# Preparing weight factors one ring entry at a time, and the position scores of the later queries as two fp32r products

## The chip, the cores and the metric

The kernel runs on one core of one Trainium2 chip. The time is device microseconds of one execution; the number that counts is the median of three runs. The core's engines, as the profile names them: PE (TensorE, matrix products; PEld is its loading of the stationary operand), DVE (VectorE), ACT (ScalarE), POOL (GpSimd) and SP (SyncE, which here only issues the DMA transfers of weights). Each engine works off its own instructions in the order in which the build wrote them.

## The reference, cut to what matters

A decoder trunk of two layers over 256 positions of width 2048, all in float32. Layer 0 mixes by a gated short convolution, layer 1 by multi-head latent attention with 16 heads; behind each stands an MLP with squared ReLU and a hidden width of 8192. A layer norm follows every sub-layer.

```python
def sq_relu_mlp(x, w1, w2):
    return jnp.square(jax.nn.relu(x @ w1)) @ w2
...
def attend_block(args):
    qn, qp, blk = args
    s = (jnp.einsum("bqhd,bkhd->bhqk", qn, k_nope)
         + jnp.einsum("bqhr,bkr->bhqk", qp, k_pe)).astype(jnp.float32) * scale
    q_pos = blk * Q_BLOCK + jnp.arange(Q_BLOCK)
    mask = k_pos[None, :] <= q_pos[:, None]
    s = jnp.where(mask[None, None], s, -jnp.inf)
    p = jax.nn.softmax(s, axis=-1).astype(v.dtype)
    return jnp.einsum("bhqk,bkhd->bqhd", p, v)
```

A score has two parts: the head's own one over 128 features (qn, k_nope), and the position part over 64 rotated features (qp, k_pe), whose keys all heads share. The queries come in two blocks of 128; the first sees at most 128 keys, the later one 256.

## The kernel before

**Precision.** Nearly all products are made in the format fp32r, and an operand is held as two tiles of it: hi, a cast of the value (ACT, L127, in `split`), and lo, the value minus hi (DVE, L128). A product of two such pairs is three fp32r products: hi by hi, hi by lo, lo by hi (`dot`, L290 to L293; `mm_k1`, L223 to L225; `high` and `low`, L205 and L209). Some small products stay full F32; one of these stands in the trace as two records.

**The weight stream.** All weights pass once, in the order of the list `stream`, as entries of 128 x 1024. An entry is loaded by SP (L138) into a raw tile, of which there are five, and split into one of eight hi/lo pairs (the ring; RAW = 5, WA = 8). `take` (L176) hands out the next entries, and before that has later ones prepared by `prepare` (L141), as long as the entries ahead count at most LOOK = 5.

**Paired factors.** The MLPs cut the second product of the hidden eighths q = 1 to 6 (FAST; twelve paired chunks over both MLPs) by a scheme of seven products in place of eight (Strassen's kind). Such a factor comes from two loads and needs three ring entries and half a one: `_1` is the first raw tile, `_t` a difference of blocks (raw_t, L160), `_2` the second tile after a further difference (L163), and t4 another (L166) in a tile of its own. Before the change, `prepare` makes all of that in one go, and the factor counts three in the look-ahead: it is begun only when all three fit.

**A paired chunk** (`down_pairs`, from L630) takes, in this order: three paired factors s0, s1, s2 (products into banks ps_r); p0 and p1, one plain entry each, taken with a look-ahead of LOOK + 1; and four paired factors f0 to f3 (84 products of 128x512 into banks ps_f). Within one factor the seven products go in the order 3, 1, 5, 7, 2, 6, 4 (`FACTORS`), each three matmuls. The running sums go in and out of PSUM by copies of ACT: `put_back` (L609) stores a ps_r bank, `resumed` (L605) fills a ps_f bank with what has been summed so far. A bank of ps_f can be filled only when the bank's earlier sum has been stored. The copies and put-backs between the last s and f0 are issued while p0 and p1 are taken.

**Attention.** The heads go in four groups of four. `project` (L880) makes a group's keys, queries, rotated queries p4 (`rope`, L807, on DVE) and values from the latent tiles; `attend` (L914) does one head in three steps: scores (L923 the head's own part, L924 the position part, both F32) with the softmax up to its scaling; transposes and a copy; the product with the values. The rotated queries of two heads share a tile of 128 rows, 64 each. The position keys kpe hold, for each of the two, 64 rows of keys and 64 rows of zeros, so that one product of 128 rows takes one head's part. `together` runs the steps of three neighbouring heads, and the group's heads are interleaved with the next group's projections. Behind the last group, the first three units of the output product (`out_first`, ps_wo) fill in: BEHIND says how many of its 16 steps follow each of the seven last calls.

What stands in which order on an engine is otherwise settled by the build's scheduler, from the order of the code and the free tiles.

Of the kernel before, what the change touches and what calls it, by code (L numbers as in the profile page):

```python
# [10 lines left out]
F32 = mybir.dt.float32  # L11
F32R = mybir.dt.float32r
AF = mybir.ActivationFunctionType
ALU = mybir.AluOpType
AX = mybir.AxisListType

P = 128
W = 256 + 2
T = 256
# [22 lines left out]
HEAD = 4  # L42
# [2 lines left out]
TURNED = 2  # L45
LAG = 8
WO_G = 3
BEHIND = (2, 2, 2, 3, 2, 2, 3)

C_G, C_B, C_CW, C_QG, C_KG, C_END = 0, 64, 128, 176, 180, 184  # L50

# [2 lines left out]
def trunk(ctx: ExitStack, tc: tile.TileContext, xT, vecs, lead, w_first, w_in, w_out, w_kv, w_q, w_uk, w_uv,  # L54
          w_qn, w_qp, w_o, w1, w2, w2f, cosT, sinT, mask, ident, gb, out):
    nc = tc.nc
# [44 lines left out]
    class Banks:  # L101
# [15 lines left out]
        @classmethod  # L117
        def next(cls):
            cls.count += 1
            return (cls.count - 1) % (4 if cls.more is None else 8)  # L120

    state = {"split": 0, "next": 0}
    ready = {}

    def split(hi, lo, src):

        nc.scalar.copy(hi, src)  # L127
        nc.vector.tensor_tensor(lo, src, hi.bitcast(F32), ALU.subtract)  # L128

    def tiled(w):  # L130
        return w.rearrange("p (b c) -> p b c", c=P)
# [9 lines left out]
    def prepare(i):  # L141

        if len(stream[i]) == 1:
            raw = load_raw(i, stream[i][0])
            hi, lo = ready[i] = parts(i)
            split(hi, lo, tiled(raw))
            return
        r1, r2 = (load_raw(f"{i}_{j}", src) for j, src in enumerate(stream[i]))
        out = []

        def finished(r, name):
            hi, lo = parts(name)
            split(hi, lo, tiled(r))
            out.append((hi, lo))

        b22, (b21, b12) = r1[:, BW:], (r2[:, :BW], r2[:, BW:])
        finished(r1, f"{i}_1")
        t = raws.tile([P, 1024], F32, tag="raw", name=f"raw{i}_t")
        two = "p (a c) -> p a c"
        nc.vector.tensor_tensor(t.rearrange(two, a=2), b12.unsqueeze(1).to_broadcast([P, 2, BW]),  # L160
                                r1.rearrange(two, a=2), ALU.subtract)
        finished(t, f"{i}_t")
        nc.vector.tensor_tensor(b12, b22, t[:, :BW], ALU.subtract)  # L163
        finished(r2, f"{i}_2")
        t4 = r1[:, :BW]
        nc.vector.tensor_tensor(t4, b21, b12, ALU.subtract)  # L166
        f = state["fast"].tile([P, 2, BW], F32R, tag="t4", name=f"t4_{i}", bufs=2)
        split(f[:, 0, :], f[:, 1, :], t4)
        b1, t13, b2 = ([[v.rearrange("p b c -> p (b c)")[:, o:o + BW] for v in w] for o in (0, BW)] for w in out)
        ready[i] = {"11": b1[0], "22": b1[1], "21": b2[0], "T2": b2[1], "T1": t13[0], "T3": t13[1],  # L170
                    "T4": [f[:, 0, :], f[:, 1, :]]}

    def size(i):

        return 1 if len(stream[i]) == 1 else 3

    def take(halves=2, look=LOOK):

        i = state["next"]
        state["next"] += halves  # L180
        ahead = -sum(size(j) for j in range(i, i + halves))
        for j in range(i, len(stream)):
            ahead += size(j)
            if ahead > look:
                break
            if j >= state["split"]:
                prepare(j)
                state["split"] = j + 1
        return [ready.pop(i + j) for j in range(halves)]

    def psum(name, bank=None):

# [331 lines left out]
    for k0, k1 in pieces:  # L524
# [5 lines left out]
        for u in range(HEAD):  # L530
            hi, lo = ready[2 * u + half]
            split(hi[:, at, :], lo[:, at, :], w[:, :, u, :])
    state["split"] = 2 * HEAD
    nc.sync.dma_start(vec, vecs)

    zt = act.tile([P, NC, 2 * T], F32R, tag="b", name="z")
# [247 lines left out]
    with tc.tile_pool(name="att", bufs=1) as ap:  # L784
# [6 lines left out]
            nc.sync.dma_start(t, source)  # L791
        kpe = ap.tile([P, 2, T], F32, name="kpe")
        nc.gpsimd.memset(kpe, 0.0)
        rc = ap.tile([P, 2], F32, name="rc")
        rk = ap.tile([P, T], F32, name="rk")
        sc = ap.tile([P, 2], F32, name="sc")
# [2 lines left out]
        def rope(dst, src, rows):  # L799

            a = tmp.tile([P, T], F32, tag="sq", name="ropea")
            b = tmp.tile([P, T], F32, tag="evac", name="ropeb")
            nc.vector.tensor_tensor(a[rows], src[rows], cos_t[rows], ALU.mult)
            for s in range(rows.start, rows.stop, 32):
                d = s ^ 32
                nc.vector.tensor_tensor(b[d:d + 32], src[s:s + 32], sin_t[s:s + 32], ALU.mult)
            nc.vector.tensor_tensor(dst[rows], a[rows], b[rows], ALU.add)  # L807
# [41 lines left out]
        f = tmp.tile([P, T], F32, tag="fh", name="fpe", bufs=3)  # L849
        ln.weighted(next(pss), f)  # L850
        for j in range(2):
            rope(kpe[:, j, :], f, slice(64 * j, 64 * j + 64))
        for m in range(NK):
            ps = next(pss)
            if m == 0:
# [22 lines left out]
        with tc.tile_pool(name="att2", bufs=2) as a2, \  # L878
                tc.tile_pool(name="paux", bufs=1, space=PS) as paux:
            def project(g, box):  # L880

                k4, q4, p4, v4 = (t[g % 2] for t in (k2, q2, p2, v2))
                box.update(k=k4, q=q4, p=p4, v=v4)
                w = take()
                for j in range(4):
                    ps = psum("ps_k")
                    mm(ps, w, 4 * j, chl, NK)
                    nc.vector.tensor_tensor(k4[:, j, :], ps[:, :T], rk, ALU.mult)
                    yield
                w = take()  # L890
                for j in range(4):
                    ps = psum("ps_q")
                    mm(ps, w, 4 * j, qhl, NK)
                    nc.scalar.copy(q4[:, j, :], ps[:, :T])
                    yield
                if g == 0:
                    query_scale()
                for _ in range(4):
                    ln.normal(next(todo))
                w = take(1)  # L900
                for j in range(2):
                    ps = psum("ps_p")
                    mm(ps, w, 4 * j, qhl, NK)
                    rope(p4[:, j, :], ps[:, :T], slice(0, P))
                    yield
                w = take()
                for b in range(2):
                    ps = psum("ps_v")
                    for k in range(NK):
                        dot(ps, wide_rows(w[k // 2], k % 2), held(chl[k], b), k == 0, k == NK - 1)  # L910
                    nc.scalar.activation(v4[:, b, :], ps, AF.Copy, scale=rc[:, b:b + 1])
                    yield

            def attend(h, box):  # L914

                j = h % 4
                qn, kn = box["q"][:, j, :], box["k"][:, j, :]
                qp, kp = box["p"][:, j // 2, :], kpe[:, h % 2, :]
                S = paux.tile([P, 512], F32, tag="S", name=f"S_{h}", bufs=2)
                spans = ((0, P), (P, T))  # L920
                for b, (at, n) in enumerate(spans):
                    tok = slice(b * P, (b + 1) * P)
                    nc.tensor.matmul(S[:, at:at + n], qn[:, tok], kn[:, :n], start=True, stop=False)  # L923
                    nc.tensor.matmul(S[:, at:at + n], qp[:, tok], kp[:, :n], start=False, stop=True)  # L924
                pr = pr2[h % 2]
                mx = small.tile([P, 2], F32, tag="mx", name="mx")
                su = small.tile([P, 2], F32, tag="su", name="su")
                nc.vector.tensor_tensor(pr, S[:, :3 * P], mask_t, ALU.add)
                for b, (at, n) in enumerate(spans):
                    nc.vector.tensor_reduce(mx[:, b:b + 1], pr[:, at:at + n], AX.X, ALU.max)  # L930
                nc.vector.tensor_tensor(mx, mx, nsc, ALU.mult)
                for b, (at, n) in enumerate(spans):
                    nc.scalar.activation(pr[:, at:at + n], pr[:, at:at + n], AF.Exp, bias=mx[:, b:b + 1],
                                         scale=sc[:, b:b + 1], accum_out=su[:, b:b + 1])
                nc.vector.reciprocal(su, su)
                for b, (at, n) in enumerate(spans):
                    nc.vector.tensor_scalar(pr[:, at:at + n], pr[:, at:at + n], su[:, b:b + 1], None, ALU.mult)
                yield
                tp = paux.tile([P, 512], F32, tag="ta", name="tp")
                for n in range(3):  # L940
                    nc.tensor.transpose(tp[:, n * P:(n + 1) * P], pr[:, n * P:(n + 1) * P], id_t)
                pt = a2.tile([P, 3 * P], F32, tag="pt", name=f"pt_{h}")
                nc.scalar.copy(pt, tp[:, :3 * P])
                yield
                po = paux.tile([P, 512], F32, tag="tb", name="po")
                vv = box["v"]
                nc.tensor.matmul(po[:, :T], vv[:, 0, j * P:(j + 1) * P], pt[:, :T], start=True, stop=False)
                nc.tensor.matmul(po[:, P:T], vv[:, 1, j * P:(j + 1) * P], pt[:, T:], start=False, stop=True)
                put_split(oT[h], po[:, :T])
                yield  # L950
# [213 lines left out]
```

## Time and profile before

| | us |
|---|---|
| median of three runs | 2004.91 |
| lowest and highest | 2004.71, 2005.23 |
| the profiled execution | 2005.16 |
| its span, first to last instruction | 2003.4 |
| granted clock of TensorE over the span | 0.999 |

The times of single instructions come from one profiled execution, 2005.16 us long, of which the span covers 2003.4. A row of a group names the line, the engine, the operation, the tiles written and read, the shape and the count; behind the bar stand the total busy time in us, the mean of one in ns, and the idle time of the engine just before these instructions with what ended most of it. A row of the timeline begins with start and length in us, counted from the span's start; in brackets is the idle time before it and what ended it. Matmuls overlap, so the step from one start to the next, not the length, is what one costs. A row of waits gives the total, the number and the longest.

### The profile page before, as it was taken

The page shows a single profiled execution, that of the slowest core. Times are in us where ns is not written, and L with a number is a line of the kernel's source. Part 1 is how long each engine was busy: PE and PEld are TensorE (multiplying, and loading weights), DVE is VectorE, ACT ScalarE, POOL GpSimd, SP SyncE. Part 2 cuts the span into 40 slices and gives each one's busy share as a digit, 9 for nine tenths or more (in the row PEclk, how much of TensorE's full clock was granted, in tenths as well). Part 3 has the DMA queues.
Part 4 walks back from the last instruction along what each step waited for, and adds up shares of the span by engine and source line. Part 5 has one row for each costly group of instructions (what it writes and reads, how often), then busy time and mean ns, then how long its engine had stood idle before and what let it go on. Part 6 is the DMA issues. An engine that isn't in the chain of part 4 may idle for free.

```text
span 2003.4 us, 30132 instructions
## 1 busy us (share of the span) xinstructions
PE 1993.4 (100%) x11114; PEld 1737.5 (87%) x11114; DVE 1715.7 (86%) x2565; ACT 1347.5 (67%) x2142; POOL 2.3 (0%) x21
## 2 busy tenths in 40 slices
PE   9999999999999999999999999999999999999998
PEld 8888888988888888888889998898888888888886
DVE  8667667788999999989978988777899999999986
ACT  6444445586877787877756755558677778887771
POOL 0000000000000000000000000000000000000000
PEclk9999999999999999999999999999999999999999
DMA  8666666564647465574854543656464646656483
GB/s 314 210 189 188 188 190 189 184 193 146 223 164 244 147 231 197 187 247 133 281 173 158 170 140 128 195 183 196 147 233 147 233 159 219 218 181 231 152 276 118
DMA packets 106851, 385.84 MB, mean 193 GB/s; under 512 B 11856, under 2 KB 12624, under 8 KB 106448
## 3 DMA queue, kind: packets, MB, share of 16 engines
q1 hardware_dynamic: 106560, 383.79, 58.8%
q8 instruction: 87, 1.43, 0.3%
q14 instruction: 60, 0.49, 0.1%
q10 hardware_dynamic: 144, 0.13, 0.0%
HBM read 381.78 MB, written 2.10 MB: 192 GB/s over the span
## 4 chain that ended last, share of the span: by engine, by line
PE 90%; DVE 7%; issue 2%; ACT 1%; DMA 0%; DVEq 0%
PE ps_u L205 21%; PE ps_l L205 13%; PE ps_u L209 11%; PE ps_l L209 7%; PE ps_r L292 4%; PE ps_r L290 4%; PE ps_r L293 4%; PE ps_d L292 3%; PE ps_d L290 3%; PE ps_d L293 3%; DVE lo L128 2%; PE ps_w L239 2%; PE ps_w L238 2%; DVE lo_t L128 2%; PE ps_w L237 2%
## 5 line engine op out<-in xcount | busy, mean ns | idle before, releaser
L128 DVE TENSOR_TENSOR lo<-raw,hi 128x1024 fp32r<-128x1024 f32 x710 | 860.5, 1219 | 191.1 <-ACT hi L127 109.4
L127 ACT CAST hi<-raw 128x1024 fp32r<-128x1024 f32 x710 | 742.3, 1051 | 241.4 <-PE ps_l L205 97.5
L205 PE MATMUL ps_u<-xhl,hi 128*128 128x512 f32 x1792 | 622.8, 393 | 0.0
L209 PE MATMUL ps_u<-xhl,lo 128*128 128x256 f32 x1792 | 498.6, 280 | 0.0
L205 PEld LDWEIGHTS ps_u<-xhl,hi 128*128 128x128 f32 x1792 | 334.5, 187 | 74.2 <-ACT acc L588 0.2
L209 PEld LDWEIGHTS ps_u<-xhl,lo 128*128 128x128 f32 x1792 | 338.2, 189 | 1.7
L205 PE MATMUL ps_l<-xhl_a,hi 128*128 128x512 f32 x704 | 244.1, 393 | 0.0
L209 PE MATMUL ps_l<-xhl_a,lo 128*128 128x256 f32 x704 | 195.4, 279 | 0.0
L205 PEld LDWEIGHTS ps_l<-xhl_a,hi 128*128 128x128 f32 x704 | 132.1, 188 | 29.9
L127 ACT CAST hi_t<-raw_t 128x1024 fp32r<-128x1024 f32 x84 | 88.6, 1055 | 84.6 <-DVE raw_t L160 69.0
L209 PEld LDWEIGHTS ps_l<-xhl_a,lo 128*128 128x128 f32 x704 | 131.9, 188 | 0.2
L160 DVE TENSOR_TENSOR raw_t<-raw,raw 128x1024 f32<-128x1024 f32 x84 | 102.2, 1217 | 2.9 <-DMA raw<-in_w2f_dram 2.9
L128 DVE TENSOR_TENSOR lo_t<-raw_t,hi_t 128x1024 fp32r<-128x1024 f32 x84 | 102.3, 1218 | 1.4 <-ACT hi_t L127 0.9
L290 PE MATMUL ps_d<-hi,h 128*128 128x512 f32 x256 | 99.9, 390 | 0.0
L292 PE MATMUL ps_d<-lo,h 128*128 128x512 f32 x256 | 99.7, 389 | 0.0
L293 PE MATMUL ps_d<-hi,h 128*128 128x512 f32 x256 | 99.7, 389 | 0.0
L205 PE MATMUL ps_l<-z,hi 128*128 128x512 f32 x240 | 82.4, 391 | 0.0
L239 PE MATMUL ps_w<-xd,hi 128*128 128x258 f32 x256 | 72.8, 284 | 0.0
L237 PE MATMUL ps_w<-xd,hi 128*128 128x258 f32 x256 | 72.3, 282 | 0.0
L238 PE MATMUL ps_w<-xd,lo 128*128 128x258 f32 x256 | 72.3, 282 | 0.0
L205 PE MATMUL ps_l<-oT,hi 128*128 128x512 f32 x208 | 71.3, 391 | 0.0
L704 ACT ACTIVATE fp<-fp 128x256 f32<-128x256 f32 x96 | 40.0, 417 | 43.9 <-DVE fp L348 43.1
(286 smaller groups left out, 3890.5 us busy)
## 6 DMA issues: line engine op xcount, KB each, us to landing
raw<-in_w_dram SPq DMA_DIRECT2D x344, 512.0 KB, 4.5
raw<-in_w2f_dram SPq DMA_DIRECT2D x168, 512.0 KB, 4.0
raw<-in_w_in_dram SPq DMA_DIRECT2D x88, 512.0 KB, 4.2
raw<-in_w_out_dram SPq DMA_DIRECT2D x32, 512.0 KB, 3.7
raw<-in_w_o_dram SPq DMA_DIRECT2D x32, 512.0 KB, 4.1
raw<-in_w_kv_dram SPq DMA_DIRECT2D x10, 512.0 KB, 4.3
raw<-in_w_q_dram SPq DMA_DIRECT2D x8, 512.0 KB, 4.2
raw<-in_w_uk_dram SPq DMA_DIRECT2D x8, 512.0 KB, 3.9
```

The costliest lines, as they stand in the source:

```text
L127: nc.scalar.copy(hi, src)
L128: nc.vector.tensor_tensor(lo, src, hi.bitcast(F32), ALU.subtract)
L160: nc.vector.tensor_tensor(t.rearrange(two, a=2), b12.unsqueeze(1).to_broadcast([P, 2, BW]), r1.rearrange(two, a=2), ALU.subtract)
L205: nc.tensor.matmul(ps, w[blk // 8][0][:, blk % 8, :], x, start=first, stop=False)
L209: nc.tensor.matmul(ps[:, :T], w[blk // 8][1][:, blk % 8, :], x[:, :T], start=False, stop=last)
L237: nc.tensor.matmul(ps[:, :W], hi, x[k][:, :W], start=k == 0, stop=False)
L238: nc.tensor.matmul(ps[:, :W], lo, x[k][:, :W], start=False, stop=False)
L239: nc.tensor.matmul(ps[:, :W], hi, x[k][:, W:], start=False, stop=k == NC - 1)
L290: nc.tensor.matmul(ps, x[0], w[0], start=first, stop=False, skip_group_check=onto)
L292: nc.tensor.matmul(ps[:, at], x[0], w[1][:, at], start=False, stop=False, skip_group_check=onto)
L293: nc.tensor.matmul(ps, x[1], w[0], start=False, stop=last, skip_group_check=onto)
L704: nc.scalar.activation(f, f, AF.Relu)
```

## The change

It has three parts.

1. `prepare` becomes a generator that stops after each ring entry, and `take` counts the look-ahead by entries: a paired factor is begun as soon as its first entry fits, and carried on entry by entry. What is begun is kept in a dictionary.
2. For the later query block, the F32 position product is replaced by two fp32r products. A new tile s4 holds, for each head, hi of the rotated queries in the head's own 64 rows, and lo in the other 64. It is multiplied by kph, in which both halves of the rows hold hi of the keys (hi by hi and lo by hi in one product), and by kpl, lo of the keys in the head's own rows and zeros in the others (hi by lo). The first block keeps its F32 product.
3. BEHIND moves a step of the output product from the fourth call to the sixth.

```diff
-BEHIND = (2, 2, 2, 3, 2, 2, 3)
+BEHIND = (2, 2, 2, 2, 2, 3, 3)
...
             split(hi, lo, tiled(raw))
+            yield
             return
...
         finished(r1, f"{i}_1")
+        yield
         t = raws.tile([P, 1024], F32, tag="raw", name=f"raw{i}_t")
...
         finished(t, f"{i}_t")
+        yield
         nc.vector.tensor_tensor(b12, b22, t[:, :BW], ALU.subtract)
         finished(r2, f"{i}_2")
...
+        yield
...
+    begun = {}
...
         for j in range(i, len(stream)):
-            ahead += size(j)
-            if ahead > look:
-                break
-            if j >= state["split"]:
-                prepare(j)
-                state["split"] = j + 1
-        return [ready.pop(i + j) for j in range(halves)]
+            for step in range(size(j)):
+                ahead += 1
+                if ahead > look:
+                    return [ready.pop(i + k) for k in range(halves)]
+                if j < 2 * HEAD:
+                    continue
+                steps = begun.setdefault(j, [prepare(j), 0])
+                if steps[1] == step:
+                    next(steps[0])
+                    steps[1] += 1
+        return [ready.pop(i + k) for k in range(halves)]
...
+        kph = ap.tile([P, T], F32R, name="kph")
+        kpl = ap.tile([P, 2, T], F32R, name="kpl")
+        nc.gpsimd.memset(kpl.bitcast(F32), 0.0)
...
         for j in range(2):
-            rope(kpe[:, j, :], f, slice(64 * j, 64 * j + 64))
+            rows = slice(64 * j, 64 * j + 64)
+            rope(kpe[:, j, :], f, rows)
+            split(kph[rows], kpl[rows, j, :], kpe[rows, j, :])
...
                     rope(p4[:, j, :], ps[:, :T], slice(0, P))
+                    for e in range(2):
+                        own, other = slice(64 * e, 64 * e + 64), slice(64 - 64 * e, 128 - 64 * e)
+                        src, hi = p4[own, j, P:], s4[own, 2 * j + e, :]
+                        nc.scalar.copy(hi, src)
+                        nc.vector.tensor_tensor(s4[other, 2 * j + e, :], src, hi.bitcast(F32), ALU.subtract)
...
-                    nc.tensor.matmul(S[:, at:at + n], qp[:, tok], kp[:, :n], start=False, stop=True)
+                    if b == 0:
+                        nc.tensor.matmul(S[:, at:at + n], qp[:, tok], kp[:, :n], start=False, stop=True)
+                    else:
+                        nc.tensor.matmul(S[:, at:at + n], box["s"][:, j, :], kph, start=False, stop=False)
+                        nc.tensor.matmul(S[:, at:at + n], box["s"][:, j, :], kpl[:, h % 2, :], start=False, stop=True)
```

More of the change, by code (lines that the diff above doesn't have):

```diff
@@ L120, in next @@
             return (cls.count - 1) % (4 if cls.more is None else 8)
-    state = {"split": 0, "next": 0}
+    state = {"next": 0}
     ready = {}
@@ L532, in trunk @@
             split(hi[:, at, :], lo[:, at, :], w[:, :, u, :])
-    state["split"] = 2 * HEAD
     nc.sync.dma_start(vec, vecs)
@@ L882, in project @@
                 k4, q4, p4, v4 = (t[g % 2] for t in (k2, q2, p2, v2))
-                box.update(k=k4, q=q4, p=p4, v=v4)
+                s4 = a2.tile([P, 4, P], F32R, tag="s4", name=f"s4_{g}")
+                box.update(k=k4, q=q4, p=p4, v=v4, s=s4)
                 w = take()
```

## The prediction

> **What bounds the kernel now.** I read the page's heads first, then what PE waited for, then the windows of the stretches in which it waited.
>
> ```profile
> span 2003.4 us, 30132 instructions
> PE 1993.4 (100%) x11114; PEld 1737.5 (87%) x11114; DVE 1715.7 (86%) x2565; ACT 1347.5 (67%) x2142; POOL 2.3 (0%) x21
> ...
> PE 90%; DVE 7%; issue 2%; ACT 1%; DMA 0%; DVEq 0%
> ```
> ```profile
> PE ps_f L292 <- DVE lo_t L128: 2.4, 3, 1.0
> ```
> ```profile
> L292 PE MATMUL ps_f<-lo_t,forms 128*128 128x512 f32 x96 | 38.6, 402 | 3.2 <-DVE lo_t L128 2.4
> L290 PE MATMUL ps_f<-hi_t,forms 128*128 128x512 f32 x96 | 37.6, 392 | 0.3 <-ACT hi_t L127 0.3
> ```
>
> TensorE sets the end: 1993.4 of 2003.4 us busy. So an edit counts only by taking matmul time away or by ending a wait of PE. One wait repeats: the ps_f products, in the paired chunks of the MLPs, wait for lo_t, the low part of a factor's middle ring entry. How much it costs is best read from the twelve stretches of ps_f products, one for each paired chunk (the fields are window, its length, PE busy with the count of matmuls, clock, DMA share, GB/s):
>
> ```profile
> 514.80:541.80 27.00, 19.20 (x84) 1.00 0.63 226
> 598.00:625.00 27.00, 19.77 (x84) 1.00 0.56 177
> 682.80:709.80 27.00, 19.50 (x84) 1.00 0.57 191
> ...
> 933.80:960.80 27.00, 19.94 (x84) 1.00 0.54 171
> ...
> sum 324.00, PE 234.13; mean PE 19.51
> ```
>
> The same 84 matmuls take 19.20 in the first stretch and more in the third. A matmul that is held shows part of its wait as busy time, so the excess is 234.13 − 12 × 19.20 = 3.7, plus the idle 3.2 + 0.3 of the two groups above: **7.2 us in all**. The clock is 1.00 everywhere; only waiting explains it. The third stretch is the common form, an excess of 0.3 busy and about 0.1 idle; the second and the one at 933.80 are the large ones (about 1.6 and 2.0 with their idle).
>
> Where the wait comes from shows in VectorE and ScalarE of the third stretch:
>
> ```profile
> 682.27 1.22 DVE L160 TENSOR_TENSOR raw_t<-raw,raw 128x1024 f32<-128x1024 f32 x1
> 683.52 0.69 DVE L163 TENSOR_TENSOR raw<-raw,raw_t 128x512 f32<-128x512 f32 x1
> 685.79 1.22 DVE L128 TENSOR_TENSOR lo<-raw,hi 128x1024 fp32r<-128x1024 f32 x1 [1.57 <-PE ps_r L292]
> ...
> 700.72 1.22 DVE L128 TENSOR_TENSOR lo_t<-raw_t,hi_t 128x1024 fp32r<-128x1024 f32 x1
> ```
> ```profile
> 682.16 1.65 ACT L605 COPY ps_f<-sums 128x512 f32<-128x512 f32 x3
> 683.72 1.09 ACT L609 COPY acc<-ps_r 128x512 f32<-128x512 f32 x2
> 684.67 1.08 ACT L127 CAST hi<-raw 128x1024 fp32r<-128x1024 f32 x1
> 685.62 1.09 ACT L127 CAST hi_t<-raw_t 128x1024 fp32r<-128x1024 f32 x1
> ```
> ```profile
> 701.48 0.39 PE L290 MATMUL ps_f<-hi_t,forms 128*128 128x512 f32 x1
> 701.99 0.50 PE L292 MATMUL ps_f<-lo_t,forms 128*128 128x512 f32 x1
> ```
>
> VectorE idles 1.57 us ahead of 685.79, the first split of factor f1. The page blames PE; the timing says ScalarE: the cast that feeds the split starts at 684.67, behind three copies into ps_f and two put-backs. After that VectorE never rests until 700.72, where it makes lo_t of f3 and is about 0.3 too late (701.48 to 701.99 where 0.23 is the undisturbed step). A factor costs VectorE four operations of 1.14 (1.22 with 0.08 of overlap) and three of about 0.65, 6.5 in all, while PE uses one up in 19.20 / 4 = 4.8; so whatever VectorE loses ahead of f1 arrives at f3.
>
> **The change, part 1: factors by one ring entry.** The look-ahead now fills to the entry, so f1's first two entries are asked for before the copies. The built order says what that moves. On ScalarE: copy into ps_f1, cast f1_1, cast f1_t, two ps_f copies, two put-backs (r2, r4), cast f1_2, cast t4, put-backs r22 and r3. On VectorE the subtraction that starts f2 (raw_t) moves ahead of f1's third split. SyncE's loads and PE's products stay in place here, and nothing is added, so the cost is only in the moves.
>
> Step by step in the third stretch. Five copies fill 682.16 to 684.67, 0.50 each; a cast takes 0.95 (684.67 to 685.62). Cast f1_1 now ends at 682.16 + 0.50 + 0.95 = 683.6. VectorE is then held by its own L163, whose successor could start at 683.52 + 0.7 = 684.2. The split moves from 685.79 to 684.2: gain 1.57, all of the idle time. Next on VectorE: two splits at 1.14, the t4 subtraction at 0.6 (687.1), then raw_t of f2, which needs f2's second load:
>
> ```profile
> L138 SPq DMA_DIRECT2D raw<-in_w2f_dram x1: 327/327/327, 682.4 to 682.4; - x1
> ...
> DMA to landing us min/median/max: 5.1/5.1/5.1
> ```
>
> It lands at 682.4 + 5.1 = 687.5 and gives 0.4 back. So lo_t of f3 comes 1.2 earlier; it was 0.4 late; **the stall goes, with 0.75 spare**. VectorE's other work is no smaller, it only starts sooner.
>
> The two large stretches have less to gain:
>
> ```profile
> 602.14 1.23 DVE L128 TENSOR_TENSOR lo<-raw,hi 128x1024 fp32r<-128x1024 f32 x1 [1.33 <-ACT hi L127]
> ...
> 938.34 1.22 DVE L128 TENSOR_TENSOR lo<-raw,hi 128x1024 fp32r<-128x1024 f32 x1 [1.33 <-ACT hi L127]
> ```
>
> Idle there is 1.33; against 1.6 and 2.0 about 0.3 and 0.7 remain. Everything that is late next is the put-back of r22, now behind two casts and t4: in the third stretch 682.16 + 0.50 + 2 × 0.95 + 4 × 0.50 + 0.95 + two steps of 0.5 = 688.5. PE needs that bank at the product "4" of f0:
>
> ```profile
> 689.92 0.39 PE L290 MATMUL ps_f<-t,h 128*128 128x512 f32 x1
> ```
>
> Slack 1.4, so nothing in the eight common stretches (ps_f5 and ps_f7 shift by 1.9 and are ready at 685.1 and 685.6, before the third and fourth products). In the two large stretches I take it as covered by the 0.3 and 0.7 already left standing. Part 1: −7.2 + 1.0 = **−6.2**. Bounds: −7.2, if nothing is left; above, 0, if no stall goes (rivals).
>
> **Part 2: the position scores of the later query block.** Per head one full F32 128x256 product (L924) becomes two fp32r products of 128x256. The trace has no fp32r product of these tiles; the nearest rows follow it immediately:
>
> ```profile
> 1151.56 0.59 PE L924 MATMUL S<-kpe,kqva 128*128 128x256 f32 x2
> 1151.80 0.47 PE L223 MATMUL ps_k<-lat,lo 128*128 128x256 f32 x1
> 1152.11 0.28 PE L224 MATMUL ps_k<-lat,hi 128*128 128x256 f32 x1
> 1152.23 0.29 PE L225 MATMUL ps_k<-lat,hi 128*128 128x256 f32 x1
> ```
>
> An F32 product is two records. From its start to L224 are 0.55, which hold it and one fp32r product at 0.12 (1152.11 to 1152.23): 0.43 for the pair. The new pair is 2 × 0.12 = 0.24. Saved: 0.19 × 16 heads = **−3.1**, from −3.2 at the best to 0, if a change of number format on PE costs what it saves. I take the near end, because PE is full here and the same step from F32 to fp32r stands in the rows.
>
> Added: for each head a cast and a subtraction of 64x128 (32 instructions), two splits of 64x256, and one fill on POOL, which has nothing else. Nearest rows by size:
>
> ```profile
> L127 ACT CAST hi<-lead 128x128 fp32r<-128x128 f32 x16 | 3.6, 294 | 0.0
> ```
> ```profile
> L128 DVE TENSOR_TENSOR lo<-lead,hi 128x128 fp32r<-128x128 f32 x16 | 3.6, 283 | 0.0
> ```
>
> So about 16 × 0.28 + 2 × 0.4 = 5.3 on VectorE and as much on ScalarE, over 110 us. VectorE looks full there (columns: PE, PEld, DVE, ACT, POOL busy, clock, DMA share, GB/s), but PE is as full and does not wait for it:
>
> ```profile
> 1100.00:1130.00 30.00, 30.00 (x226) 28.88 (x225) 29.70 (x65) 19.67 (x35) 0.00 (x0) 1.00 0.65 212
> 1130.00:1240.00 110.00, 109.98 (x736) 101.91 (x736) 93.40 (x240) 67.78 (x155) 0.00 (x0) 1.00 0.37 120
> ```
>
> VectorE is ahead, preparing weights, and in the second window it has 16.6 us free: the 5.3 are covered by that. Without the cover they cost up to 5.3. The tightest place is the first group:
>
> ```profile
> 1121.09 0.42 DVE L807 TENSOR_TENSOR kqva<-ropea,ropeb 128x256 f32<-128x256 f32 x1
> ```
> ```profile
> 1124.19 0.59 PE L924 MATMUL S<-kpe,kqva 128*128 128x256 f32 x2
> ```
>
> Rotation done at 1121.5; two heads' splits one after the other, 2 × (0.29 + 0.28) = 1.15, end at 1122.7: slack 1.5. I count 0.
>
> The row on fp32r steps has a rule against it. The Trainium skill ("TensorE: Matmul & The Clock Gate", part 3, "The mechanism", the list of what overlaps) says that a weight load overlaps a running matmul only where their row groups differ; here all 128 rows are used, so each added product would show its load. By that rule part 2 would be a loss (third rival); the trace disagrees with it in ps_k, where loads of 0.19 disappear in steps of 0.12.
>
> **Part 3: BEHIND.** The sum stays at 17. In the built order five output units plus one product stand before the last head's final part in both versions, as three and two before and two and three after. A unit is three products of 512 and three of 256, 3 × (0.23 + 0.12) = 1.05, and moving one past a wait costs or gains at most that. I take **0**, bounds ±1.05.
>
> **Sum.** 2003.4 − 6.2 − 3.1 = 1994.1. The profiled execution took 2005.16, so 1.76 lie around the span: 1995.9. It stands 0.25 above the median of 2004.91, so on the median's scale **1995.6 us**. This case's own range is 1993.8 to 1999.2 (all of the stall and half of BEHIND below; above, half the attention gain gone and a further 0.2 per stretch left).
>
> **The rivals.**
>
> *ScalarE's row is longer than I add up* (0.07). If r22 comes 2.0 later than 688.5, it holds product "4" by 0.6 in the eight common stretches: 4.8, **2000.4**. For it: two casts now stand ahead of that put-back, and each waits for VectorE. Against: the 1.4 of slack.
>
> *VectorE blocked by f2's load* (0.05), the slow side. The subtraction for f2 now stands ahead of f1's third split; if its load is late, all four factors are. Spare 0.75 beyond 5.1 means that it starts to cost at 5.9 us from issue to landing, and each microsecond more costs ten in ten stretches. It is slower by 0.2% from (2008.9 − 1995.6) / 10 + 5.9 = 7.2 us on; at 7.7 it gives **2013.6**. For it, the longest landing of the stage; against, the median of these loads:
>
> ```profile
> DMA to landing us min/median/max: 3.3/4.3/7.7
> ```
> ```profile
> raw<-in_w2f_dram SPq DMA_DIRECT2D x168, 512.0 KB, 4.0
> ```
>
> *The new products show their weight loads* (0.03): a pair then takes 2 × (0.19 + 0.12) = 0.62 in place of 0.43, so +3.0 where I have −3.1: **2001.7**. For it, PEld's own duration; against, that loads of the same length vanish in the steps of 0.12 above:
>
> ```profile
> L224 PEld LDWEIGHTS ps_k<-lat,hi 128*128 128x128 f32 x64 | 12.2, 191 | 0.2
> ```
>
> *The order gains nothing* (0.06): VectorE starts f1 earlier but waits again for a cast further on, and lo_t is as late as before. Only part 2 is left: **2001.8**. For it: VectorE and ScalarE hand each factor over four times (three entries and t4); against: ScalarE has over 30% free.
>
> **Chances.** The forecast has 0.79. This kernel's measurement can tell about 0.2% from no change: faster means below 2000.9, slower above 2008.9. Faster: 0.79 and 0.04 of the first rival, 0.83; same: 0.03 + 0.03 + 0.06 = 0.12; slower 0.05. The range 1993.8 to 2000.6 takes in the first rival's middle and leaves out 0.06 + 0.03 + 0.05 and half of the first, under 0.2.
>
> **What would show it.** In the profile after, each window of ps_f should have 19.2 to 19.3 busy, with about 19.5 and 19.9 left at 598 and 933 at the most; the wait for lo_t should fall from 3.2 to under 1; VectorE's idle time before f1's first split should vanish. The position row of 128x256 should read as two products 0.12 apart. A new wait of ps_f for ACT's put-back, or of VectorE for the load of f2, would show the first or second rival. It is wrong if ps_f still has 19.5 in the common stretches.

## The result, and the profile after

The changed kernel takes 1999.24 us (median of 7 runs, 1998.47 to 2000.01), the one before 2004.71 in the same comparison (7 runs, 2003.03 to 2006.03): a ratio of 0.9973, with a 95% interval of 0.9964 to 0.9983. That is 5.5 us, where the prediction had 9.3, and 3.6 above its forecast of 1995.6. The prediction names two upper ends: the time lies 0.04 over the one of its own case, 1999.2, and inside the one that also takes in the first rival, 2000.6. The profiled execution took 1998.59, its span is 1996.8, 6.6 under the span before. Of the two parts that were to pay, one did and one hardly did.

The heads of the page, and what PE waits for now (engine, operation, what it waited for; total in us, times, longest):

```profile
span 1996.8 us, 30215 instructions
PE 1987.7 (100%) x11114; PEld 1736.6 (87%) x11114; DVE 1720.5 (86%) x2583; ACT 1355.6 (68%) x2160; POOL 2.7 (0%) x22
```
```profile
PE po L972 <- DVE oT L363: 2.2, 3, 1.1
PE offset L1083 <- DVE udiag L1081: 1.2, 1, 1.2
...
PE ps_f L300 <- ACT acc L618: 0.4, 1, 0.4
```

The wait of ps_f for lo_t has left the list; one of 0.4 for a put-back is new, and one of 2.2 in the attention: the product po (probabilities by values) waits for VectorE's oT.

The twelve windows of ps_f, with the fields as before:

```profile
...
681.00:708.00 27.00, 19.20 (x84) 1.00 0.63 226
...
930.80:957.80 27.00, 19.75 (x84) 1.00 0.57 192
...
sum 324.00, PE 231.19; mean PE 19.27
```

The reckoning of before, 231.19 − 12 × 19.20 + 0.4, leaves 1.2 of 7.2 us: **the factor part gained 6.0**. What the move did is seen in the third stretch, on ScalarE and VectorE:

```profile
680.23 0.61 ACT L614 COPY ps_f<-sums 128x512 f32<-128x512 f32 x1
680.75 1.07 ACT L127 CAST hi<-raw 128x1024 fp32r<-128x1024 f32 x1
681.70 1.06 ACT L127 CAST hi_t<-raw_t 128x1024 fp32r<-128x1024 f32 x1
682.65 1.12 ACT L614 COPY ps_f<-sums 128x512 f32<-128x512 f32 x2
...
686.12 1.10 ACT L618 COPY acc<-ps_r 128x512 f32<-128x512 f32 x2
```
```profile
681.15 0.69 DVE L166 TENSOR_TENSOR raw<-raw,raw_t 128x512 f32<-128x512 f32 x1
681.85 1.23 DVE L128 TENSOR_TENSOR lo<-raw,hi 128x1024 fp32r<-128x1024 f32 x1
...
696.54 1.22 DVE L128 TENSOR_TENSOR lo_t<-raw_t,hi_t 128x1024 fp32r<-128x1024 f32 x1
```
```profile
688.12 0.39 PE L300 MATMUL ps_f<-t,h 128*128 128x512 f32 x1
```

The casts of f1_1 (680.75) and f1_t stand right behind the copy at 680.23, ahead of the other two copies and of the put-backs. VectorE goes from L166 (L163 before) to f1's first split without a pause. lo_t of f3 starts at 696.54 and is done by 697.8; PE uses it at 699.91. The put-back of r22 (the first of the two from 686.12) is done 1.4 before PE starts the product "4" at 688.12.

The attention: how long the products po take, from the first head's to the last one's. The first row is the kernel before, the second the changed one:

```profile
L947 PE MATMUL po<-pt,kqva x32: 377/378/454, 1140.5 to 1233.3; 128*128 128x256 f32 x32
```
```profile
L972 PE MATMUL po<-pt,kqva x32: 377/378/455, 1135.8 to 1228.9; 128*128 128x256 f32 x32
```

1233.3 − 1140.5 = 92.8 before, 93.1 after. The scores of thirteen heads lie in this stretch, those of three ahead of it; thirteen should have taken 13 × 0.19 = 2.5 off it, and instead it is 0.3 longer. What they saved on PE was there. One head's scores, before (first fence, with the rows of the prediction) and after:

```profile
1151.12 0.60 PE L923 MATMUL S<-kqva 128*128 128x256 f32 x2
```
```profile
1146.24 0.60 PE L944 MATMUL S<-kqva 128*128 128x256 f32 x2
1146.49 0.47 PE L948 MATMUL S<-kph,s 128*128 128x256 f32 x1
1146.80 0.29 PE L949 MATMUL S<-kpl,s 128*128 128x256 f32 x1
1146.92 0.28 PE L233 MATMUL ps_k<-lat,lo 128*128 128x256 f32 x1
1147.04 0.28 PE L234 MATMUL ps_k<-lat,hi 128*128 128x256 f32 x1
```

From the head's own part to the second ps_k product are 1152.11 − 1151.12 = 0.99 before and 1147.04 − 1146.24 = 0.80 after: 0.19 a head, as predicted. The two new products start 0.31 apart, not 0.12 as the prediction had it; but before the change the first two products behind the F32 pair read so too (1151.80 and 1152.11), so only the sum over these rows tells. The saving went back to the waits of po. Where the first of them arises, on VectorE and PE:

```profile
1175.43 1.22 DVE L128 TENSOR_TENSOR lo<-raw,hi 128x1024 fp32r<-128x1024 f32 x1
1176.68 0.60 DVE L924 TENSOR_TENSOR s<-kqva,s 64x128 fp32r<-64x128 f32 x2
1177.32 2.36 DVE L128 TENSOR_TENSOR lo<-raw,hi 128x1024 fp32r<-128x1024 f32 x2
1179.71 0.42 DVE L363 TENSOR_TENSOR oT<-po,oT 128x256 fp32r<-128x256 f32 x1
```
```profile
1179.36 0.28 PE L235 MATMUL ps_k<-lat,hi 128*128 128x256 f32 x1
1180.28 0.67 PE L972 MATMUL po<-pt,kqva 128*128 128x256 f32 x2 [0.64 <-DVE oT L363]
```

The product po has one PSUM bank. Before it can be written for the next head, VectorE must have read it for the low part of oT, and that subtraction stands behind three weight splits and the new pair (L924). At the same head before the change, two weight splits stood there, and po did not wait:

```profile
1179.86 2.35 DVE L128 TENSOR_TENSOR lo<-raw,hi 128x1024 fp32r<-128x1024 f32 x2
1182.24 0.42 DVE L353 TENSOR_TENSOR oT<-po,oT 128x256 fp32r<-128x256 f32 x1
```
```profile
1185.30 0.60 PE L947 MATMUL po<-pt,kqva 128*128 128x256 f32 x2
```

There the subtraction starts 3.06 ahead of the product. In the changed kernel PE was due for the product one step after 1179.36, at 1179.48, and the subtraction starts 0.23 behind that: it is 3.3 later, counted from when PE needs it.

The 2.2 of idle are not the whole price, since a held product shows part of its wait as busy time: the pair of po is recorded at 0.67 where it was held and at 0.60 before the change. By the stretch the waits cost 0.3 + 2.5 = 2.8.

And VectorE is not short of time (columns: PE, PEld, DVE, ACT, POOL busy, clock, DMA share, GB/s):

```profile
1130.00:1240.00 110.00, 107.78 (x725) 99.46 (x725) 98.15 (x252) 72.51 (x169) 0.00 (x0) 1.00 0.37 116
```

Before, PE had 109.98 and VectorE 93.40 here: VectorE does 4.8 more and still has 11.9 free, and PE idles 2.2 more.

### The profile page after: what moved, and what is told of

The parts are those of the page before. It is cut to its first block, busy times and chain, and to the rows that moved or that the text cites. A ratio compares the mean times of both kernels' runs of the same rounds, so it can differ in the third digit from the quotient of the medians.

```text
span 1996.8 us, 30215 instructions
## 1 busy us (share of the span) xinstructions
PE 1987.7 (100%) x11114; PEld 1736.6 (87%) x11114; DVE 1720.5 (86%) x2583; ACT 1355.6 (68%) x2160; POOL 2.7 (0%) x22
## 4 chain that ended last, share of the span: by engine, by line
PE 94%; DVE 5%; ACT 1%; issue 1%; DVEq 0%; ACTq 0%
PE ps_u L215 20%; PE ps_l L215 13%; PE ps_u L219 10%; PE ps_l L219 7%; PE ps_f L300 4%; PE ps_f L302 4%; PE ps_f L303 4%; PE ps_r L302 4%; PE ps_r L303 4%; PE ps_r L300 4%; PE ps_d L300 3%; PE ps_d L302 3%; PE ps_d L303 3%; PE ps_w L249 2%; PE ps_w L248 2%; PE ps_w L247 2%
```

## The experiments

The theory (A): the factor part took away the stall of ps_f and touched nothing else; the scores save some 3 us on PE, but the splits they add on VectorE delay its reading of the po bank, and PE waits. The rivals B to F stand in the expectations, each with what it would show.

**The factor part alone.** The changed kernel with the scores and BEHIND of before.

```diff
+BEHIND = (2, 2, 2, 3, 2, 2, 3)
...
-            split(kph[rows], kpl[rows, j, :], kpe[rows, j, :])
...
-                        nc.scalar.copy(hi, src)
-                        nc.vector.tensor_tensor(s4[other, 2 * j + e, :], src, hi.bitcast(F32), ALU.subtract)
...
+                    nc.tensor.matmul(S[:, at:at + n], qp[:, tok], kp[:, :n], start=False, stop=True)
```

> Only the preparation by ring entry is taken over; scores and BEHIND stay as before. Theory A (the factor part took the stall of ps_f away and touched nothing else): 6.0 us under before, each ps_f window at 19.2 busy but the one near 935 (about 1.0 left), no wait of the product po for oT. Rival B (the new order of take also moves weight splits ahead of oT in the attention, and that makes PE wait there): about 3.6 us under before, with 2.2 us of wait of po for oT.

Measured: 2000.43 against 2004.93, ratio 0.9979 (0.9970 to 0.9987), so 4.5 us with the interval from 2.6 to 6.0, where 6.0 was expected. In its profile neither po nor the transposes wait, and the stretch of po is 1229.3 − 1136.5 = 92.8, as before. What is left in ps_f is 1.8 (231.62 busy, 0.6 idle, most of it one wait of 0.5 for the put-back), against 1.2 in the changed kernel.

So the attention's waits do not come from the factors (B falls), and most of the gain does.

**The scores alone.** The kernel before with part 2 of the change.

```diff
+            split(kph[rows], kpl[rows, j, :], kpe[rows, j, :])
...
+                        nc.scalar.copy(hi, src)
+                        nc.vector.tensor_tensor(s4[other, 2 * j + e, :], src, hi.bitcast(F32), ALU.subtract)
...
+                        nc.tensor.matmul(S[:, at:at + n], box["s"][:, j, :], kph, start=False, stop=False)
+                        nc.tensor.matmul(S[:, at:at + n], box["s"][:, j, :], kpl[:, h % 2, :], start=False, stop=True)
```

> Only the position scores are taken over. Theory A (16 x 0.19 saved on PE, but the added splits of the rotated queries push the low part of oT back on VectorE, behind weight splits, and the next product po waits 2.2 to 2.4 us in all): 0.7 us under before, with waits of po for oT; the waits for lo_t stay at 3.2. Rival B (the waits come from the factor part): 3.1 us under before and no wait of po.

Measured: 2003.74 against 2004.93, ratio 0.9995 (0.9986 to 1.0004): no difference that can be told from none. Its list of waits has both:

```profile
PE ps_f L292 <- DVE lo_t L128: 2.9, 4, 1.0
PE po L963 <- DVE oT L353: 2.2, 3, 1.1
```

The same 2.2, three times, at the same heads, with the old factors and the old BEHIND, and a stretch of 1233.0 − 1139.9 = 93.1. The scores bring their waits along.

**BEHIND alone.**

```diff
-BEHIND = (2, 2, 2, 3, 2, 2, 3)
+BEHIND = (2, 2, 2, 2, 2, 3, 3)
```

> Only BEHIND changes. Theory A: within 0.3 us of before, since PE's next work at the moved step was ready anyway. Rival: up to 1.05 us either way, one unit of the output product on the wrong side of a wait.

Measured: 2004.28 against 2004.93, ratio 0.9996 (0.9987 to 1.0005). The stretch of po is 1231.1 − 1138.3 = 92.8, as before, and nothing waits in it.

**Two halves of one bank for po.**

```diff
-                po = paux.tile([P, 512], F32, tag="tb", name="po")
+                po = po2[0][:, T * (h % 2):T * (h % 2 + 1)]
...
+            po2 = [paux.tile([P, 512], F32, tag="tb", name="po")]
```

> The changed kernel, but the products po of even and odd heads lie in the two halves of one PSUM bank, so that a head's po need not wait until the low part of the head before has been read out. Theory A (po waits only for its own bank): 2.2 us under the changed kernel, no wait of po for oT. Rival C (VectorE has too little time in the attention, so the wait only moves to the scores' softmax or to the weights): no change, within 0.5 us of the changed kernel, and a new wait of PE of about 2 us.

Measured: 1999.51, ratio 0.9976 (0.9966 to 0.9986), and the wait of po is unchanged at 2.2. Theory A missed, but the run does not speak against it: po waits at the same three heads as in the changed kernel, so the two halves did not free it from VectorE. Presumably the dependence is kept for the whole tile; no run shows that by itself. The next run gives the heads separate banks.

**Banks in turn.** A head's transposes and po share a bank, and heads alternate.

```diff
-                tp = paux.tile([P, 512], F32, tag="ta", name="tp")
+                tp = paux.tile([P, 512], F32, tag=("ta", "tb")[h % 2], name="tp")
...
-                po = paux.tile([P, 512], F32, tag="tb", name="po")
+                po = paux.tile([P, 512], F32, tag=("ta", "tb")[h % 2], name="po")
```

> The changed kernel, but a head's transposes and its product po share one PSUM bank and even and odd heads take the two banks in turn (before, all transposes had one bank and all po the other). By the wait lists po then no longer waits for VectorE. Theory A (the new waits of 2.2 us are the reuse of the one po bank, released by the late low part of the head before): no wait of po, PE fully busy from 1130 to 1240, span 2.2 us shorter than the changed kernel's 1996.8, about 1994.6. Rival C (VectorE is short of time there and the wait moves to the transposes or to the weights): 0.5 us at most, and a new wait of about 2 us on another product.

Measured: 2000.07, ratio 0.9976 (0.9966 to 0.9985); span 1997.2, not 1994.6. The wait for oT moved:

```profile
PE tp L966 <- DVE oT L363: 0.7, 1, 0.7
...
PE po L972 <- ACT pt L968: 0.4, 1, 0.4
PE tp L966 <- DVE kqva L962: 0.3, 1, 0.3
```

Of the idle time in the attention 1.4 are left of 2.2, but the stretch is 1229.1 − 1136.1 = 93.0, only 0.1 shorter than in the changed kernel:

```profile
L972 PE MATMUL po<-pt,kqva x32: 377/378/483, 1136.1 to 1229.1; 128*128 128x256 f32 x32
```

The transposes that follow po are the next to use the bank which VectorE is late to read, so the wait came one product later; it shows 0.7 of idle where the longest had been 1.1, and now the scaled scores (kqva), which VectorE also makes, show as well. Theory A missed: a second bank hardly shortens the stretch while VectorE is late. The time is the one that C expected (0.5 at most), and the wait moved as C had it; the cause that C names is not seen, since 11.8 us of VectorE's 110 are free here too.

**No low part of the queries.** Without the 16 subtractions; those rows hold zeros, so this part of the scores is left out.

```diff
-                        nc.vector.tensor_tensor(s4[other, 2 * j + e, :], src, hi.bitcast(F32), ALU.subtract)
...
+                nc.gpsimd.memset(s4.bitcast(F32), 0.0)
```

> The changed kernel without the 16 subtractions that make the low part of the rotated queries of the later block (these rows hold zeros instead), so that part of the scores is left out; PE's products and the 16 casts stay. Theory A: in the order as built, one weight split less stands between the last scaling of the scores and the low part of oT, and the 0.6 us of a pair's subtractions are gone, so po waits under 0.4 us in all: 2 us under the changed kernel. Rival D (the casts on ScalarE, or the order of the weight splits by themselves, make po late): the waits of 2.2 us stay.

Measured: 1998.77, ratio 0.9969 (0.9957 to 0.9981). The stretch of po is 1227.2 − 1135.5 = 91.7, 1.4 shorter than in the changed kernel. The wait of po is 1.0, not 2.2. Counting the heads from 0, the changed kernel waits at heads 6, 10 and 14; here heads 6 and 10, where the subtractions had stood ahead of oT, do not wait at all, head 14 keeps its 0.45, and head 11 has a new wait of 0.51. VectorE at the place shown above, head 6:

```profile
1174.38 1.22 DVE L128 TENSOR_TENSOR lo<-raw,hi 128x1024 fp32r<-128x1024 f32 x1
...
1176.11 0.42 DVE L363 TENSOR_TENSOR oT<-po,oT 128x256 fp32r<-128x256 f32 x1 [0.51 <-ACT oT L362]
```

The low part of oT starts at 1176.11, not 1179.71, with one weight split ahead of it where three stood. Of these 3.6, 0.3 are PE's own: it starts the product at 1179.15 here, where it was due at 1179.48. So a pair of subtractions of 0.60 goes with 3.3 us of lateness: the order that the scheduler writes changes with it. That is more than the theory said. Less is that 1.0 of idle remains, by the stretch 1.4 of the 2.8. At head 14 three weight splits and no subtraction stand ahead of oT, with and without the edit. What makes these two waits is open: D (casts, or the order of the weight splits by itself) can claim them, and so can PE, which comes to each head earlier than before.

**The subtractions on POOL.**

```diff
-                        nc.vector.tensor_tensor(s4[other, 2 * j + e, :], src, hi.bitcast(F32), ALU.subtract)
+                        nc.gpsimd.tensor_tensor(s4[other, 2 * j + e, :], src, hi.bitcast(F32), ALU.subtract)
```

> The changed kernel with those 16 subtractions on POOL in place of VectorE. Theory A: like the run without them, po waits under 0.4 us and the time is 2 us under the changed kernel, unless POOL takes over 3 us for one, when the first scores of a group wait for them. Rival D: the waits of 2.2 us stay.

Measured: 1998.80, ratio 0.9971 (0.9961 to 0.9980). po waits 0.9, at heads 11 and 14 as without the subtractions, and the stretch is 1229.5 − 1137.9 = 91.6; one subtraction takes POOL 0.95 us, and no score waits for it:

```profile
L924 POOL TENSOR_TENSOR s<-kqva,s 64x128 fp32r<-64x128 f32 x16 | 15.3, 953 | 200.9 <-ACT s L923 200.3
```

Its profiled execution, 2002.56 and the longest of its nine, also shows how much the remaining wait in ps_f varies, with the same code in the MLPs:

```profile
PE ps_f L300 <- ACT acc L618: 2.0, 5, 0.5
...
PE po L972 <- DVE oT L363: 0.9, 2, 0.5
PE ps_f L302 <- DVE lo_t L128: 0.9, 1, 0.9
PE ps_f L300 <- ACT ps_f L614: 0.7, 2, 0.4
```

By the reckoning of the windows that is 6.3 us of excess (233.06 busy, 3.6 idle), against 1.2 in the changed kernel's profile and 0.2 (230.56 busy, none idle) in that of the run without the subtractions.

**The whole factor early.** The kernel before, with a look-ahead of 7 at p0 and p1.

```diff
-                    w, = take(1, LOOK + 1)
+                    w, = take(1, LOOK + 2)
```

> The kernel before, but the two plain entries ahead of f0 are taken with a look-ahead of 7 in place of 6, so that the whole of f1 is prepared ahead of the copies, not two of its entries. Theory A (all of the stall was the cast of f1_1 behind copies and put-backs): the stall of ps_f goes here too, from 7.2 to about 1 us, unless the third entry's cast holds up the copies that fill ps_f: 1 to 6 us under before, with new waits of ps_f for ScalarE. Rival E (stopping after each entry matters by itself): no gain, the waits for lo_t stay at about 3.

Measured: 2000.97 against 2004.96, ratio 0.9982 (0.9972 to 0.9991). The stall for lo_t is gone, and the expected new one is there: 3.7 us of excess in the windows (231.65 busy, 2.4 idle), all of the idle time for ScalarE's copies into ps_f.

```profile
PE ps_f L290 <- ACT ps_f L605: 2.4, 4, 0.7
```
```profile
683.60 0.61 ACT L605 COPY ps_f<-sums 128x512 f32<-128x512 f32 x1
684.12 1.06 ACT L127 CAST hi<-raw 128x1024 fp32r<-128x1024 f32 x1
685.21 1.06 ACT L127 CAST hi_t<-raw_t 128x1024 fp32r<-128x1024 f32 x1
686.17 1.04 ACT L127 CAST hi<-raw 128x1024 fp32r<-128x1024 f32 x1
687.11 1.10 ACT L605 COPY ps_f<-sums 128x512 f32<-128x512 f32 x2
```

Three casts stand ahead of the copies, and PE comes for ps_f5 before 687.11 ends. E falls: the stall for lo_t goes without stopping after each entry. It is ScalarE's row that decides, and the third cast is one too many there. How much stopping after two entries is worth over this is open: the factors alone took 2000.43, and the intervals of the two overlap.

**Both remedies.** POOL's subtractions and the banks in turn, the edits as above.

> The changed kernel with the 16 subtractions on POOL and with the two PSUM banks taken in turn by even and odd heads. In the runs with one of these two, PE still waited in the attention for 1.0 us (POOL) and 1.4 us (banks) in place of 2.2. Theory A (VectorE reads the bank of po late, because of the added work and of weight splits that stand ahead of it; each remedy takes a part of that): together under 0.5 us of wait of po and of the transposes, the attention about 2 us shorter than in the changed kernel. Rival C (VectorE is short of time there): about 1 us left, as with POOL alone.

Measured: **1997.49** against 2004.45, ratio 0.9967 (0.9954 to 0.9979), the lowest median of all. po and the transposes wait 0.7 in all, over the expected 0.5, and none of it is for oT:

```profile
PE po L972 <- ACT pt L968: 0.4, 1, 0.4
...
PE tp L966 <- DVE kqva L962: 0.3, 1, 0.3
```
```profile
L972 PE MATMUL po<-pt,kqva x32: 377/378/483, 1135.5 to 1227.0; 128*128 128x256 f32 x32
```

The stretch of po is 91.5, 1.6 shorter than in the changed kernel and 1.3 shorter than before. POOL alone has 91.6, so the banks add 0.1: in time this is what C expected (as with POOL alone), and the remedy is the place of the subtractions. The run beats the kernel before clearly; against the changed kernel the intervals overlap, and only the profile's stretch tells them apart.

**Six raw tiles.** One load more in flight, one ring pair less. What suggested it: in the changed kernel, the stretch from 933.75, which keeps the largest excess, has two loads some 50 us ahead of it that land 6.4 and 6.3 us after issue, where the same loads ahead of the stretch from 850.5, with no excess, took 4.2 and 4.6; from there on VectorE runs about 1.5 us later.

```diff
-RAW, WA = 5, 8
+RAW, WA = 6, 7
```

> The changed kernel with six raw tiles in place of five and seven ring pairs in place of eight, as space allows no more. Theory A (what is left of the wait in ps_f, 0 to 1.5 us in some chunks, comes from loads that land 2 us late some 45 us earlier, after which VectorE does not catch up): with a load more in flight the excess over all ps_f windows is under 0.5 us, if seven pairs are enough for a look-ahead of 5. Rival F (the ring is what holds the factors): the pairs are short, PE waits for lo and hi in ps_f and ps_r, and the kernel is over 5 us slower than the changed one.

Measured: 2002.78 against 2004.45, ratio 0.9991 (0.9982 to 1.0000). Neither theory is borne out. The excess in ps_f is 1.4 (231.60 busy, 0.2 idle), as in the changed kernel, and there are no waits for the ring. The time was lost in the last microseconds of the kernel. The first products into offset (L1078) start at 1986.12 here and at 1985.89 in the changed kernel, so 3.4 of the 3.6 by which the span is longer come after that; one wait there has grown from 1.2:

```profile
PE offset L1083 <- DVE udiag L1081: 3.0, 1, 3.0
```

What the late loads contribute to the rest in ps_f stays open, and so does why the end grew.

## Why the prediction was right, and where not

**What bounds, and part 1: right.** The stall was 7.2, its cause the cast of f1_1 behind ScalarE's copies, and the move took away 6.0 of it where 6.2 was forecast. f1's first split gained more than the 1.57 of idle time: it starts 2.2 us ahead of the stretch's first product (684.04) where it started 0.05 ahead of it, because what precedes it on VectorE came earlier too. So lo_t of f3 is 2.1 ahead of need, not 0.75. The slack of r22, put at 1.4, is 1.4. That two or so stretches would keep something was right, but one of the two names was not: the second kept nothing here, the one at 933 did, and the excess moves between executions and stretches.

**Part 2: the size on PE right, the cover wrong.** 0.19 a head was saved (3.04 in all, which the prediction rounds to 3.1), and no weight load showed. The step that failed is "the 5.3 are covered by that" for VectorE's 16.6 free microseconds, and with it the term of −3.1 to be counted in full. The free time is there, but a total says nothing of the order. PE waits for one subtraction, oT's, that releases the only bank of po, and with the added work a third weight split and the new pair stand ahead of it. The prediction looked at the new splits' own latest use (slack 1.5 in the first group, and there nothing waited), not at what stands behind them on VectorE. With 2.8 given back, part 2 is worth about 3.0 − 2.8 = 0.2 us, which the run of it alone cannot tell from nothing. Half of the 2.8 went with the subtractions' place on VectorE (1.4 and 1.5 in the two runs that took them off it); the cause of the other half is not shown.

**BEHIND: right**, 0 within what can be measured.

**The sum.** 2003.4 − 6.0 = 1997.4 against a span of 1996.8. So the changed kernel is the factor part with little else: part 2's 0.2 leave 0.4, which lie within the scatter of single executions. Of the 3.6 by which the forecast was low, 2.9 are the attention's term and 0.2 the factors'. That the time still lies in the wider range is partly luck: the range had room for half of the attention gain, and nearly all of it went, while the stretches kept little more than forecast (1.2 against 1.0). The range's lower end is mis-added: all of the stall and half of BEHIND below 1995.6 give 1994.1, not 1993.8.

**The rivals.** ScalarE's row: in part, in one stretch of the profiled execution. There the product "4" comes late by 0.44 for the put-back of r22, which is the mechanism described:

```profile
938.68 0.50 PE L300 MATMUL ps_f<-t,h 128*128 128x512 f32 x1 [0.44 <-ACT acc L618]
```

Its slack of 1.4 holds for the common stretches only; where the stream of factors is late by over a microsecond, it is the first thing to give. VectorE blocked by f2's load: not seen; over the whole kernel VectorE waits 1.9 us for the loads that raw_t needs, 2.9 before. The weight loads: not seen, L949 to L233 is 0.12 apart, with loads recorded at 0.19. The rule of the Trainium skill ("TensorE: Matmul & The Clock Gate", part 3, "The mechanism"), by which a load overlaps only a product of other row groups, does not hold for these products of all 128 rows. The same section of the Trainium skill also has loads into a background weight buffer pulled ahead of running products, and with that the trace agrees. That the order gains nothing: wrong.

## What to carry to other kernels

Free time of an engine covers added work only if nothing that the bounding engine needs stands behind it: before costing an addition at nothing, list what follows it on its engine and which PSUM bank or tile that releases. An added pair of 0.6 us made a release 3.3 us late, with the different order that the scheduler wrote around it. Price a wait by the stretch that it lies in, not by the idle time alone: 2.2 of idle were 2.8 us here, and with the banks in turn the idle time fell by 0.8 and the stretch by 0.1. A prefetch that is begun in parts can fill a gap that a whole one misses, and one part too many (the third cast, here) turns the same gap into a new wait.

## What the hardware showed that was not expected

The waits that are left in the MLPs are not the same from one profile to the next: 0.2, 1.2, 1.8 and 6.3 us of excess in four profiles with the same factor code (the run without subtractions, the changed kernel, the factors alone, POOL). The edits between these runs lie in the attention, behind the first six stretches, and up to 1000 us PE, VectorE and ScalarE work off the same instructions in the same order in all four traces; yet the busy excess of these six is already 0.14, 0.58, 0.75 and 1.27. So a single profile prices such a residue badly. The cause of that scatter was not settled.
